# A layer with mLSTM recurrence on one core: the running maxima as rows through DRAM, a mask on GpSimd, and longer load estimates in the planner

## Chip, cores and metric

The kernel runs on one core of a Trainium2 chip. The metric is the device time of one execution in microseconds. The median of three runs is shown, and beside it the time of the one execution that the hardware profiler recorded. The engines are called TensorE (PE; its weight loads PEld), VectorE (DVE), ScalarE (ACT), GpSimd (POOL) and SyncE (SP), whose queue issues the DMA transfers.

## What is computed

One layer over 2048 tokens of width 1024 in float32, followed by a final norm. Two token mixers work side by side on one input projection: attention over a band of chunks (8 heads of 64), and an mLSTM, a matrix memory with exponential gates (4 heads of 128). Their outputs are gated and projected, and a feed-forward part of width 4096 follows. The change lies in the mLSTM. The part of the reference that matters, for one head:

```python
g = bcum + m_st[:, :, None]
dmat = bcum[:, :, :, None, :] - bcum[:, :, None, :, :] + ig[:, :, None, :, :]
dmat = jnp.where(causal[None, None, :, :, None], dmat, -jnp.inf)
m_t = jnp.maximum(g, jnp.max(dmat, axis=3))
dw = jnp.exp(dmat - m_t[:, :, :, None, :])
qk = jnp.einsum('bcthd,bcshd->bctsh', q, k) * dw
inter = jnp.exp(g - m_t)
num = (inter[..., None] * jnp.einsum('bchvk,bcthk->bcthv', c_st, q)
       + jnp.einsum('bctsh,bcshv->bcthv', qk, v))
den = inter * jnp.einsum('bchk,bcthk->bcth', n_st, q) + jnp.sum(qk, axis=3)
hout = num / jnp.maximum(jnp.abs(den), jnp.exp(-m_t))[..., None]
```

The weights `dw` form a triangle over source token s and target token t. After the cumulative sum of the target's forget gates cancels, each weight is the exponential of u(s) - m(t), where u belongs to the source and m is the target's running maximum.

## The kernel before

Tokens are worked in four blocks of 512 (`NB = 4`, `T = 512`), each cut into four chunks of 128 (`NT = 4`); the mLSTM uses chunks of 128 with the same result. Tiles hold features on the partitions and the 512 tokens of a block along the free dimension. Large products are made in three matmuls from operands that ScalarE and VectorE split into a high and a low part (L583 and L585 for weights, L1224 and L1229 for activations). Many of them are done as quads, a seven-product scheme for 2 by 2 blocks (L727), the others in the plain way (L644 to L646).

The program is written by a planner. Each piece of work is a Python generator, a thread, that yields requests: "pe", "act", "dve", "pool" or "sp" with an estimated duration (and, for transfers, an estimated time to landing), "get" for tiles of a pool, "wait" for events. `Flow.run` (L174) plays these threads against clocks of the engines and emits each instruction when its turn comes. The order in which TensorE's instructions are emitted is final. For threads with a priority below 5, TensorE's start is put `SLACK` = 800 ns behind the moment they are ready; the thread of the dense products has priority 5 and fills the list between them. Afterwards `Order` (L225) replays the whole program with its own durations and due times and settles the order on the other engines, SP's queue included. Each engine then executes its list in order; an instruction that waits holds up all that stands behind it.

The mLSTM of one block b goes as follows.

- `gates_rest` (L1493) makes, for 4 chunks x 4 heads, the sums of the gates, the sources' u (`sm["u"]`), the running maxima (`sm["mt"]`, 128 tokens x 16 columns) and their exponentials `ex`. At its end four transposes (L1580) bring the maxima into rows, a head to a partition, and a copy and a subtraction (L1582, L1585) split them into two parts in `mtt`. Then the event `gates` is set.
- `recurrence_far` (L1589) starts the heads; two are under way at most (`rec_room`). Each takes two tiles from `rpool`, two from `ctx` (the second of a head's tiles, `w`, holds the weights) and one from `temp`.
- `load_rec` (L1608) loads k, q and the values mv of a head, one after the other in the planner's reckoning (L1618, L1622).
- `rec_head` (L1655) waits for `gates`. It makes the exponents in a PSUM bank by two matmuls: L1663 puts the triangle's mask into it (identity times a bfloat16 mask), L1664 subtracts the maximum of each target by means of a column of `nsel` that picks the head's row of `mtt`. Four exponentials (L1668) read the bank, with u as the bias, and write `w`. Then come the transposes of k (L1675), its scaling by ScalarE (L1679), the products of k and q (L1686), their product with `w` on VectorE (L1688), and for each chunk three matmuls with the values and the state (L1700 to L1702) and the state's update (L1705).
- A square root is a power on GpSimd (L1722). GpSimd further scales the output gates of blocks 0 and 1 (L1652) and sets the edges of the attention's bias (L1324, L1325), and little else.

The recurrences of blocks 0 and 1 lie beside the input projections of these blocks, those of blocks 2 and 3 beside the first down projection; there they share tiles and banks with attention. The mixers' outputs go to DRAM (`mixd`, `mixa`), and `take_mix` (L961) brings them back for the projection (L989). A row is already spread over all partitions in other places: `row_out` (L1117) stores it to DRAM, and `row_in` (L1131) loads it with a source whose partition step is zero.

Of the kernel before, what the change touches and what calls it, by code (L numbers as in the profile page):

```python
# [30 lines left out]
P = 128  # L31
# [185 lines left out]
def dve_ns(n):  # L217
    return 70 + 1.042 * n
# [154 lines left out]
class Layer:  # L373
# [8 lines left out]
    def make_tiles(self, pool, psum):  # L382
# [8 lines left out]
        self.temp = Pool([f32(f"tmp{i}", 516) for i in range(6)])  # L391
# [6 lines left out]
        self.identb = pool.tile([P, P], BF16, name="identb")  # L398
        self.maskb = pool.tile([P, 1, P], BF16, name="maskb")
        self.gw = f32r("gw", KT + 4, 16)  # L400
        self.sel = f32("sel", 8)
# [7 lines left out]
        self.mtt = f32r("mtt", T)  # L409
        self.nsel = f32r("nsel", 8)  # L410
# [26 lines left out]
    def setup_late(self):  # L437
# [12 lines left out]
        nc.vector.memset(raw[:, :512], 0.0)  # L450
        nc.vector.tensor_copy(self.mtt, raw[:, :512])
        fl.put(self.temp, raw)
        yield "sp", 300, 2200
        nc.sync.dma_start(self.sel, io["sel"])
# [6 lines left out]
        nc.vector.tensor_copy(self.identb, self.ident)  # L461
        nc.vector.tensor_scalar(self.maskb[:, 0], self.tri, 1.0, -NEG, op0=ALU.subtract, op1=ALU.mult)
        nc.vector.tensor_scalar(self.nsel, self.sel, -1.0, None, op0=ALU.mult)
# [1029 lines left out]
    def gates_rest(self, b):  # L1493
# [84 lines left out]
        yield "pe", 428  # L1578
        for c in range(NT):
            nc.tensor.transpose(bk[:MH, c * P:(c + 1) * P], sm["mt"][:, c * MH:(c + 1) * MH], self.ident)  # L1580
        yield "act", act_ns(512, True)
        nc.scalar.copy(self.mtt[:MH], bk[:MH])  # L1582
# [25 lines left out]
    def load_rec(self, b, h):  # L1608
# [46 lines left out]
    def rec_head(self, b, h):  # L1655
# [5 lines left out]
        (bk,) = yield "get", self.banks, 1  # L1661
        yield "pe", 440
        mm(bk.rearrange("p (c t) -> p c t", c=NT), self.identb, self.maskb.to_broadcast([P, NT, P]), start=True, stop=False)  # L1663
        mm(bk, self.nsel[:, h:h + 1].to_broadcast([P, P]), self.mtt, start=False, stop=True)  # L1664
        for c in range(NT):
            n = c * MH + h
            yield "act", act_ns(128, True, 1)
            nc.scalar.activation(w[:, c * P:(c + 1) * P], bk[:, c * P:(c + 1) * P], AF.Exp,  # L1668
                                 bias=self.sm["u"][:, n:n + 1])
        fl.put(self.banks, bk)  # L1670
# [779 lines left out]
    def build(self):  # L2450
# [17 lines left out]
        self.rowd = {n: f32d("row" + n, T) for n in ("in1", "in2", "in3", "mid0", "mid1", "mid2", "mid3", "out0", "out1", "out2")}  # L2468
        self.wi = 0
# [17 lines left out]
        for b in range(NB):  # L2487
# [3 lines left out]
                gates=Event(), mv_slots=Event(), mv_ev=E(NT), ctx={}, mvh={}, ctx_ev=E(MH), qk_ev=E(2 * MH), og_ev=E(MH),  # L2491
# [14 lines left out]
def _layout(np, p):  # L2506
# [37 lines left out]
    sel = np.zeros((P, 8), np.float32)  # L2544
    for j in range(8):
        sel[j, j] = sel[32 + j, j] = 1.0
# [10 lines left out]
        sel=sel,  # L2557
# [29 lines left out]
```

## Time and profile before

| | us |
|---|---|
| median of three runs | 2779.6 (2778.0 to 2780.48) |
| the profiled execution | 2778.32 |
| its span, first to last instruction | 2776.5 |
| TensorE busy | 2751.0, 12994 matmuls |
| VectorE busy | 2057.1 |
| ScalarE busy | 1494.5 |
| GpSimd busy | 53.7 |

The granted TensorE clock was 0.998 of full speed. A row of a group reads: line, engine, operation, written tile, arrow, read tiles, shapes, count, then busy time, mean duration of one in ns, and the idle time of the engine just before these instructions. Matmuls overlap in such records, so a matmul's price in the stream is the distance from its start to the next start, not its duration. A row of the timeline reads: start, duration, engine, line, operation, tiles, count, and in brackets the idle time before it and what ended it. A row of the windows has the length of the stretch, the busy time of each engine with its number of instructions, the granted clock, the share of the DMA engines and the GB/s. For one line or tile the three numbers are the shortest, middle and longest duration in ns.

### The profile page before, as it was taken

To read this page: it belongs to the slowest core of one execution; us is meant where nothing else is said; L and a number is where in the kernel's file an instruction comes from. 1 tells how busy PE (TensorE), PEld (TensorE's weight loads), DVE (VectorE), ACT (ScalarE), POOL (GpSimd) and SP (SyncE) were. 2 spreads that over 40 slices of the span, in tenths; PEclk is the share of its full clock that TensorE was granted. 3 is DMA by queue.
4 is the path that set the end of the run, shared out by engine and by line. 5 is a ranking of instruction groups with operands and counts; after the bars stand their busy time and mean duration, and the time that the engine had idled before them with its cause. 6 is when DMAs were issued, how large, how long until landed. Compare 5 with 4: busy or idle time off the path is not lost.

```text
span 2776.5 us, 38600 instructions
## 1 busy us (share of the span) xinstructions
PE 2751.0 (99%) x12994; PEld 2286.5 (82%) x12994; DVE 2057.1 (74%) x3783; ACT 1494.5 (54%) x2608; POOL 53.7 (2%) x100
## 2 busy tenths in 40 slices
PE   9999999999999999999999999999999999999998
PEld 7888888888778878888888888888888888888887
DVE  7796789768996866886676688789888656556565
ACT  5564576535453535575555556565436655554443
POOL 0010001000000000000000000000000000000000
PEclk9999999999999999999999999999999999999999
DMA  7958759769755667579877887788777567666564
GB/s 273 291 195 276 230 166 304 250 222 319 262 199 204 220 243 256 198 270 325 288 280 273 287 245 233 230 256 253 251 261 261 206 220 261 243 238 217 189 230 149
DMA packets 329046, 678.64 MB, mean 244 GB/s; under 512 B 36840, under 2 KB 67728, under 8 KB 328848
## 3 DMA queue, kind: packets, MB, share of 16 engines
q1 hardware_dynamic: 328848, 676.18, 72.3%
q8 instruction: 102, 1.67, 0.2%
q14 instruction: 96, 0.79, 0.1%
HBM read 472.59 MB, written 203.44 MB: 243 GB/s over the span
## 4 chain that ended last, share of the span: by engine, by line
PE 91%; DMA 3%; DVE 3%; issue 2%; ACT 1%; SPq 0%; POOLq 0%; POOL 0%; DVEq 0%; ACTq 0%
PE bank L727 43%; PE bank L644 12%; PE bank L645 12%; PE bank L646 12%; PE bank L1415 2%; PE bank L1388 2%; PE bank L1446 2%; PE bank L755 2%; DVE wsp L585 1%; PE bank L1700 1%; PE bank L1701 1%; PE bank L1702 0%; PE bank L1686 0%; DMA wsum<-ctx 0%; ACT wsp L583 0%
## 5 line engine op out<-in xcount | busy, mean ns | idle before, releaser
L727 PE MATMUL bank<-r,wsp 128*128 128x512 f32 x5544 | 1265.5, 390 | 1.4 <-DVE ctx L1867 0.6
L727 PEld LDWEIGHTS bank<-r,wsp 128*128 128x128 f32 x5544 | 1038.0, 188 | 222.5 <-DVE ctx L1867 3.8
L585 DVE TENSOR_TENSOR wsp<-wraw,wsp 128x1024 fp32r<-128x1024 f32 x459 | 561.6, 1224 | 360.9 <-ACT wsp L583 335.2
L583 ACT CAST wsp<-wraw 128x1024 fp32r<-128x1024 f32 x459 | 482.5, 1052 | 464.1 <-PE bank L727 209.0
L644 PE MATMUL bank<-r,wsp 128*128 128x512 f32 x1472 | 586.1, 398 | 2.3 <-ACT r L1224 2.1
L645 PE MATMUL bank<-r,wsp 128*128 128x512 f32 x1472 | 574.8, 391 | 0.2 <-DVE r L1229 0.2
L646 PE MATMUL bank<-r,wsp 128*128 128x512 f32 x1472 | 574.9, 391 | 0.0
L646 PEld LDWEIGHTS bank<-r,wsp 128*128 128x128 f32 x1472 | 276.3, 188 | 58.7
L644 PEld LDWEIGHTS bank<-r,wsp 128*128 128x128 f32 x1472 | 276.9, 188 | 54.0 <-ACT r L1224 2.3
L645 PEld LDWEIGHTS bank<-r,wsp 128*128 128x128 f32 x1472 | 277.0, 188 | 50.5 <-DVE r L1229 0.5
L1867 DVE TENSOR_TENSOR ctx<-bank,ctx 128x512 f32<-128x512 f32 x186 | 127.1, 688 | 89.4 <-PE bank L727 89.2
L1229 DVE TENSOR_TENSOR r<-r 128x512 fp32r<-128x512 f32 x248 | 163.9, 687 | 25.3 <-ACT r L1224 24.5
L1224 ACT CAST r<-r 128x512 fp32r<-128x512 f32 x248 | 147.8, 624 | 49.8 <-DMA r<-u 47.0
L1859 ACT COPY ctx<-bank 128x512 f32<-128x512 f32 x186 | 107.9, 581 | 64.5 <-PE bank L727 60.9
L1430 ACT ACTIVATE sc<-sc,scs 128x640 f32<-128x640 f32 (+4 forms) x128 | 97.5, 763 | 71.7 <-DVE scs L1427 65.6
L2198 ACT ACTIVATE ctx<-ctx 128x512 f32<-128x512 f32 x96 | 60.6, 631 | 102.6 <-DVE ctx L1867 102.6
L1451 DVE TENSOR_TENSOR r<-bank,r 128x512 fp32r<-128x512 f32 (+1 forms) x168 | 97.1, 597 | 16.5 <-ACT r L1449 15.7
L1449 ACT CAST r<-bank 128x512 fp32r<-128x512 f32 (+1 forms) x168 | 81.8, 518 | 47.9 <-PE bank L1446 46.0
L1421 DVE CUSTOM_DVE_ANT_0 sc<-bank,bias 128x320 f32<-128x320 f32 (+3 forms) x240 | 103.7, 463 | 3.6 <-PE bank L1415 2.6
L1388 PE MATMUL bank<-r,r 128*128 128x512 f32 x336 | 96.0, 367 | 2.8 <-DVE r L1451 2.6
L602 DVE TENSOR_TENSOR wraw<-wraw,wraw 128x1024 f32<-128x1024 f32 x76 | 92.9, 1223 | 2.0
L552 DVE TENSOR_TENSOR ctx<-ctx,ctx 128x512 f32<-128x512 f32 x112 | 76.5, 688 | 17.7 <-DMA ctx<-in_wf 11.7
(258 smaller groups left out, 2720.7 us busy)
## 6 DMA issues: line engine op xcount, KB each, us to landing
wraw<-in_wf SPq DMA_DIRECT2D x178, 512.0 KB, 4.0
wraw<-wsum SPq DMA_DIRECT2D x136, 512.0 KB, 4.1
r<-u SPq DMA_DIRECT2D x224, 256.0 KB, 4.3
wraw<-in_w SPq DMA_DIRECT2D x88, 512.0 KB, 5.0
u<-ctx SPq DMA_DIRECT2D x128, 256.0 KB, 2.6
ctx<-in_wf SPq DMA_DIRECT2D x112, 256.0 KB, 4.3
wsum<-ctx SPq DMA_DIRECT2D x112, 256.0 KB, 3.6
u<-tmp SPq DMA_DIRECT2D x96, 256.0 KB, 3.7
```

Source lines behind the costliest of these rows:

```text
L583: nc.scalar.copy(w[:, 0], raw)
L585: nc.vector.tensor_sub(w[:, 1], raw, w[:, 0].bitcast(F32))
L644: mm(ps, lh, rh, start=first, stop=False)
L645: mm(ps, lh, rl, start=False, stop=False)
L646: mm(ps, ll, rh, start=False, stop=last)
L727: mm(ps, wv[:, x, k, n], a[:, y], start=new and k == 0 and x == y == 0, stop=k == 3 and x == 1, skip_group_check=True)
L1224: self.nc.scalar.copy(dst[:, 0], src)
L1229: self.nc.vector.tensor_sub(dst[:, 1], src, dst[:, 0].bitcast(F32))
L1388: nc.tensor.matmul(acc[:, :, c0:c0 + w], st, sl[:, :, o:o + w], start=n == 0, stop=n == total - 1)
L1421: nc.vector.tensor_tensor_reduce(out=e[:, x * w:x * w + w], in0=bks[x][:, :w], in1=br[:, j0 + x * w:j0 + x * w + w], op0=ALU.add, op1=ALU. ...
L1859: nc.scalar.copy(t[:, o:o + 512], ps)
L1867: nc.vector.tensor_add(t[:, o:o + 512], ps, t[:, o:o + 512])
```

## The change

The exponents are no longer made by TensorE. One transpose (of the maxima, sorted by head and chunk into 16 columns) replaces four, and ScalarE copies the result, 16 rows of 128, into one of the `cum` tiles, from where it goes to a DRAM tensor `rowm`, one for each block; only then is `gates` set. A new thread for each head, `row_rec`, waits for `gates`, loads the 512 maxima of the head from there into `w`, the same row on all partitions, and GpSimd adds a mask `later`, 1e30 where the target lies ahead of the source and 0 elsewhere. The four exponentials then read `w`, with a scale of -1 and u as the bias, and write in place. They stand, as before, ahead of the transposes of k in the head's thread, and now take no PSUM bank. The estimated time to landing for the head's loads goes from 2.0 to 4.5 us in the planner, and the pool of temporaries from six tiles to seven. `mtt`, `nsel`, `sel`, `identb` and `maskb` go, with their setup.

```diff
-        self.temp = Pool([f32(f"tmp{i}", 516) for i in range(6)])
+        self.temp = Pool([f32(f"tmp{i}", 516) for i in range(7)])
...
+        nc.vector.tensor_scalar(self.later[:, 0], self.tri, NEG, -NEG, op0=ALU.mult, op1=ALU.add)
...
-        yield "pe", 428
-        for c in range(NT):
-            nc.tensor.transpose(bk[:MH, c * P:(c + 1) * P], sm["mt"][:, c * MH:(c + 1) * MH], self.ident)
-        yield "act", act_ns(512, True)
-        nc.scalar.copy(self.mtt[:MH], bk[:MH])
-        yield "dve", dve_ns(512)
-        yield "dve", 85
-        V.tensor_sub(self.mtt[32:32 + MH], bk[:MH], self.mtt[:MH].bitcast(F32))
+        yield "dve", 85
+        V.tensor_copy(p.rearrange("p (m c) -> p m c", c=NT), v4("mt").rearrange("p c m -> p m c"))
+        yield "pe", 110
+        nc.tensor.transpose(bk[:16, 384:512], p, self.ident)
+        yield "act", act_ns(P, True)
+        nc.scalar.copy(z[:, 64:], bk[:16, 384:512])
         fl.put(self.banks, bk)
+        yield "sp", 900, 2000
+        nc.sync.dma_start(self.rowm[b].ap(), z[:, 64:])
         fl.set(B["gates"])
...
             fl.spawn(self.load_rec(b, h), 1)
+            fl.spawn(self.row_rec(b, h, B["ctx"][h][3]), 1)
             fl.spawn(self.rec_head(b, h), 1)
...
-            yield "sp", 900, 2000
+            yield "sp", 900, 4500
             nc.sync.dma_start(to[:, :512], self.mfar[b].ap()[x])
...
-        yield "sp", 900, 2000
+        yield "sp", 900, 4500
         nc.sync.dma_start(mvv[:, :, :128], self.mvfar[b].ap()[:, :, h * P:(h + 1) * P].rearrange("t p c -> p t c"))
...
+    def row_rec(self, b, h, w):
+
+        fl, nc, B = self.fl, self.nc, self.blk[b]
+        yield "wait", [B["gates"]]
+        yield "sp", 900, 4500
+        nc.sync.dma_start(w[:, :T], bass.AP(self.rowm[b], h * T, [[0, P], [1, T]]))
+        yield "pool", 730
+        w4 = w[:, :T].rearrange("p (c t) -> p c t", c=NT)
+        nc.gpsimd.tensor_tensor(w4, w4, self.later.to_broadcast([P, NT, P]), op=ALU.add)
+        fl.set(B["row_ev"][h])
...
         yield "wait", [B["gates"]]
-        (bk,) = yield "get", self.banks, 1
-        yield "pe", 440
-        mm(bk.rearrange("p (c t) -> p c t", c=NT), self.identb, self.maskb.to_broadcast([P, NT, P]), start=True, stop=False)
-        mm(bk, self.nsel[:, h:h + 1].to_broadcast([P, P]), self.mtt, start=False, stop=True)
+        yield "wait", [B["row_ev"][h]]
         for c in range(NT):
             n = c * MH + h
-            yield "act", act_ns(128, True, 1)
-            nc.scalar.activation(w[:, c * P:(c + 1) * P], bk[:, c * P:(c + 1) * P], AF.Exp,
+            yield "act", act_ns(128, False, 1)
+            nc.scalar.activation(w[:, c * P:(c + 1) * P], w[:, c * P:(c + 1) * P], AF.Exp, scale=-1.0,
                                  bias=self.sm["u"][:, n:n + 1])
-        fl.put(self.banks, bk)
         yield "wait", [B["qk_ev"][MH + h]]
```

More of the change, by code (lines that the diff above doesn't have):

```diff
@@ L397, in make_tiles @@
         self.ones = f32("ones", 2)
-        self.identb = pool.tile([P, P], BF16, name="identb")
-        self.maskb = pool.tile([P, 1, P], BF16, name="maskb")
+        self.later = f32("later", 1, P)
         self.gw = f32r("gw", KT + 4, 16)
-        self.sel = f32("sel", 8)
         self.bif = f32("bif", NT, 8)
@@ L2468, in build @@
         self.rowd = {n: f32d("row" + n, T) for n in ("in1", "in2", "in3", "mid0", "mid1", "mid2", "mid3", "out0", "out1", "out2")}
+        self.rowm = [f32d(f"rowm{b}", 16, P) for b in range(NB)]
         self.wi = 0
@@ L2490, in build @@
                 kq_ev=E(AH), q_ev=E(AH), k_ev=E(AH), k_spilt=E(AH), kq_all=Event(), head_done=E(AH),
-                gates=Event(), mv_slots=Event(), mv_ev=E(NT), ctx={}, mvh={}, ctx_ev=E(MH), qk_ev=E(2 * MH), og_ev=E(MH),
+                gates=Event(), mv_slots=Event(), mv_ev=E(NT), ctx={}, mvh={}, ctx_ev=E(MH), qk_ev=E(2 * MH), row_ev=E(MH), og_ev=E(MH),
                 mix=[None] * 8, mix_ev=E(8), ga={}, ga_ev=E(8), xs_free=Event(), x_room=E(KT), mid=Event(), vo={}, vn={}, vp_ev=E(4), mvh_ev=E(MH), gf=Event(), rec_slots={}, heads_left=[2] * 4))
@@ L2543, in _layout @@
     eye = np.eye(P, dtype=np.float32)
-    sel = np.zeros((P, 8), np.float32)
-    for j in range(8):
-        sel[j, j] = sel[32 + j, j] = 1.0
     cols = lambda v: v.reshape(-1, P).T
```

9 lines of the change are left out of this document (removed).

## The prediction, made before the changed kernel ran

> **What bounds the kernel now.** I read the page first, then who made TensorE wait, then the timeline around the instructions that the change removes. The page gives the span, the busy shares and the chain that ended last:
>
> ```profile
> span 2776.5 us, 38600 instructions
> PE 2751.0 (99%) x12994; PEld 2286.5 (82%) x12994; DVE 2057.1 (74%) x3783; ACT 1494.5 (54%) x2608; POOL 53.7 (2%) x100
> PE 91%; DMA 3%; DVE 3%; issue 2%; ACT 1%; SPq 0%; POOLq 0%; POOL 0%; DVEq 0%; ACTq 0%
> ```
>
> TensorE is the bound, 91% of the chain. Its stream is one fixed list in program order, so an instruction taken out of it is worth its start-to-start time wherever TensorE isn't waiting. The other engines come second, and matter where they make that list wait. These are the waits that the trace names ahead of matmuls (total us, times, longest):
>
> ```profile
> PE bank L644 <- ACT r L1180: 6.4, 1, 6.4
> PE bank L1388 <- DVE r L1451: 2.6, 2, 2.1
> PE bank L755 <- DVE ctx L1867: 2.4, 2, 2.0
> PE bank L644 <- ACT r L1224: 2.1, 1, 2.1
> PE bank L1700 <- DMA r<-mvfar: 0.7, 1, 0.7
> PE bank L727 <- DVE ctx L1867: 0.6, 1, 0.6
> ```
>
> The first is the start of the program, which the change doesn't touch. Of the rest, only L1700 is the recurrence waiting for its own load. The others (attention, the combining of the quads, the operands of the down projection) sum to 2.6 + 2.4 + 2.1 + 0.6 = 7.7 us.
>
> **Removed: the pair of matmuls for each head (L1663, L1664).** Here is one of the 16 pairs, with start and duration in us, and the two groups:
>
> ```profile
> 1835.72 0.39 PE L1663 MATMUL bank<-maskb,identb 128*128 128x512 bf16 x1
> 1835.76 0.58 PE L1664 MATMUL bank<-mtt,nsel 128*128 128x512 f32 x1
> 1836.18 0.39 PE L644 MATMUL bank<-r,wsp 128*128 128x512 f32 x1
> 1836.40 0.39 PE L645 MATMUL bank<-r,wsp 128*128 128x512 f32 x1
> ...
> L1664 PE MATMUL bank<-mtt,nsel 128*128 128x512 f32 x16 | 9.0, 583 | 0.0
> L1663 PE MATMUL bank<-maskb,identb 128*128 128x512 bf16 x16 | 6.2, 388 | 0.0
> ```
>
> Durations overlap, so I use starts: the next matmul starts 1836.18 - 1835.72 = 0.46 us after the pair begins, and runs at the usual 0.22 us from there. The last column of both groups is 0.0: TensorE wasn't idle ahead of them, so no wait swallows the saving. 16 x 0.46 = 7.4 us off the stream.
>
> **Removed: three of the four transposes of the running maxima, in each of four blocks.** Four transposes (L1580) become one of a tile with 16 columns, as L1534 has it:
>
> ```profile
> 67.92 0.60 PE L1580 MATMUL bank<-const,g_mt 128*4 128x128 f32 x4
> 68.28 0.48 PE L644 MATMUL bank<-r,wsp 128*128 128x512 f32 x1
> 68.59 0.39 PE L645 MATMUL bank<-r,wsp 128*128 128x512 f32 x1
> ...
> 55.62 0.27 PE L1534 MATMUL bank<-const,g_u 128*16 128x128 f32 x1
> 55.64 0.48 PE L644 MATMUL bank<-wsp,r 128*128 128x512 f32 x1
> 55.96 0.39 PE L645 MATMUL bank<-wsp,r 128*128 128x512 f32 x1
> ```
>
> From the group's start to L645 it is 0.67 us with four and 0.34 with one, and the L644 between them takes about 0.23 of it either way. The difference of 0.33 us, four times, is 1.3 us. On the other engines the block loses a copy and a subtraction of 4x512 and gains two small copies. VectorE (74% busy) and ScalarE (54%) aren't the bound, so that counts as nothing for the time.
>
> **Longer estimates for a head's loads.** They move no data. They make the planner place a head's matmuls later behind its loads, 4.5 us instead of 2.0. What they can win is the stall at L1700, where the load landed late:
>
> ```profile
> 452.39 0.39 PE L646 MATMUL bank<-r,wsp 128*128 128x512 f32 x1
> 453.52 0.46 PE L1700 MATMUL bank<-r,ctx 128*128 128x129 f32 x2 [0.74 <-DMA r<-mvfar]
> ```
>
> The starts lie 1.13 us apart instead of 0.23, so 0.9 us is to be had. I count 0.7, the wait itself: the loads of this kernel land in 4 to 5 us (next fence), so 4.5 covers the middle of them, not the worst.
>
> **Added: the rows.** A store per block, a load of 256 KB per head that spreads one row over 128 partitions, an addition of 128x512 on GpSimd, and the same four exponentials, now from SBUF. None of it is TensorE's. The nearest rows (L1133 is such a spread row, and the bottom line is its time to landing):
>
> ```profile
> L1133 SPq DMA_DIRECT2D tmp<-rowmid x8: 319/382/536, 1619.8 to 2684.1; - x8
> DMA to landing us min/median/max: 3.2/5.0/6.5
> ...
> r<-mfar SPq DMA_DIRECT2D x48, 256.0 KB, 4.7
> u<-ctx SPq DMA_DIRECT2D x128, 256.0 KB, 2.6
> ...
> L1652 POOL TENSOR_SCALAR ctx<-ctx,ghead x8: 1232/1759/2126, 197.2 to 453.1; 128x512 f32<-128x512 f32 x8
> ...
> L1668 ACT ACTIVATE ctx<-bank,g_u x64: 347/372/416, 73.1 to 1837.1; 128x128 f32<-128x128 f32 x64
> ```
>
> The chain of a head is then 5.0 (load) + 1.8 (addition) + 4 x 0.37 = 8.3 us at the middle. The planner reckons 0.9 + 4.5 + 0.73 + 4 x 0.29 = 7.3, and puts 0.8 us ahead of each of TensorE's instructions for such a thread. The addition with two inputs isn't in the trace: not below L1652's 1.2 us, and I bound it by twice L1652's longest, 4.3. The worst chain is 6.5 + 4.3 + 1.7 = 12.5 us, 4.4 beyond plan and margin. What hides this is the head's own loads: k, q and mv follow one another in the planner's reckoning, 3 x 5.4 = 16.2 us, and the weights are wanted only at L1700, after the last. That cover is missing where the gates come late and the loads lie far ahead, in the last block:
>
> ```profile
> 1778.62 0.58 ACT L1582 CAST mtt<-bank 4x512 fp32r<-4x512 f32 x1 [1.07 <-PE bank L1580]
> ...
> 1782.23 0.39 PE L1663 MATMUL bank<-maskb,identb 128*128 128x512 bf16 x1
> ...
> 1794.53 0.39 PE L1700 MATMUL bank<-r,ctx 128*128 128x129 f32 x2
> ```
>
> Now it is 16 us from the maxima to the first use of the weights. The store (about 2.6 us, as u<-ctx lands), the load and the addition go in between, and the planner moves these two heads' matmuls back; dense work fills the list meanwhile. Late by up to 4.4 us each, that is 0 to 9 us, and I take 0, since the middle exceeds the plan by 1.0 against a margin of 0.8. The 16 loads and 4 stores are 20 x 0.38 = 8 us of SP's issuing over the whole span, and the row's load is queued there behind the store that it must await, with all later transfers behind it. Spread rows exist already (L1133), and no matmul's wait in the list above names them. In GpSimd's queue the addition stands ahead of the power L1722 and the edges of the attention bias (L1324, L1325), and whoever waits for these waits for a late row too; I count nothing, GpSimd being 2% busy. ScalarE's exponentials, which awaited TensorE before, now await GpSimd. Behind them in ScalarE's list stand the copies of the weights (L583), for which VectorE's L585 and then the dense matmuls wait: a late row reaches TensorE on this way too, unless the three weight buffers ahead cover it.
>
> **The transfers' price where DMA is full.** In one stage it is:
>
> ```profile
> 1498.00:1560.00 62.00, 59.71 (x281) 49.23 (x281) 32.58 (x54) 31.36 (x58) 1.01 (x1) 1.00 1.01 336
> ```
>
> The DMA share is 1.01 (second last) at 336 GB/s, and TensorE loses 2.3 us, most of it the L644 wait for r behind a late load. The first two heads of block 2 load here. Two rows of 256 KB at 336 GB/s are 1.6 us. Bounds: 0 if the rows come before the crowd, 1.6 if they delay the load that TensorE awaits. I take 1.6, as nothing is free there.
>
> **Sum**, against the profiled execution of 2778.3 us (span 2776.5 and 1.8 around it): 2778.3 - 7.4 - 1.3 - 0.7 + 1.6 = 2770.5. That execution is 1.3 us below the median of the runs, 2779.6, so the forecast for a median is 2771.8, say 2772.
>
> **The rivals.**
> *The rows come late at every head (slower).* Place: L1700 (through L1688's product) of all 16 heads, in a list that can't overtake. For it: the addition's price is unknown and its plan (0.73 us) is below anything L1652 shows. Against it: 16.2 us of loads beside 7.3. The forecast's 7.8 us are gone from 0.5 us per head, and it is slower by more than can be told from no change from 0.8. L1652's middle and longest lie 1.0 and 1.4 us over the plan. If the margin is already spent on the loads, that is 16 to 22 us, 19 in the middle: 2791. Chance 0.13.
>
> *Attention finishes late.* Heads that stay longer hold tiles and PSUM banks that attention of blocks 2 and 3 wants, and their last tile has little slack ahead of the projection that ends at 2070.7:
>
> ```profile
> 2021.42 0.69 DVE L1229 TENSOR_TENSOR r<-tmp,r 128x512 fp32r<-128x512 f32 x1
> ...
> 2070.73 183.03 PE bank L727 x807
> ```
>
> Block 3's projection is 64 products of 0.68 us, 44 us, so it starts near 2027 and wants this fourth tile at 2029; it is ready at 2022.1. Slack 6 to 7 us. With a head in the last block some 7.5 us longer (3 x 2.5), two in a row 15, the end could slip by 15 and cost 8: 2780. Against it: the recurrence takes no bank for its mask any more, and one more tile in the temporaries' pool. Chance 0.09.
>
> *GpSimd holds VectorE up.* While GpSimd ran L1652, a subtraction that takes 1.22 us took 1.60:
>
> ```profile
> 215.30 3.56 POOL L1652 TENSOR_SCALAR ctx<-ctx,ghead 128x512 f32<-128x512 f32 x2 [9.27 <-ACT ctx L1649]
> ...
> 216.17 1.60 DVE L585 TENSOR_TENSOR wsp<-wraw,wsp 128x1024 fp32r<-128x1024 f32 x1
> ...
> L585 DVE TENSOR_TENSOR wsp<-wraw,wsp x459: 1214/1225/1600, 5.1 to 2746.4; 128x1024 fp32r<-128x1024 f32 x153
> ```
>
> At 0.38 us for each of 16 additions, all of it reaching TensorE, it is 6 us: 2778. VectorE's 26% idle speaks against all of it reaching TensorE. Chance 0.07. The Trainium skill, "SBUF — State Buffer", section "Who interferes with whom", says that a VectorE instruction with two SBUF inputs and a GpSimd instruction that reads SBUF exclude each other for the whole instruction. By that rule VectorE could be held for a whole addition each time, an estimate of 16 x 1.76 = 28 us, and 2800 if all of it reached TensorE; the 1.60 agrees in direction, with 0.38 us held instead of 1.76.
>
> *The order is drawn anew.* Every edit changes the planner's list for the whole program, so the 7.7 us of stalls elsewhere come out differently: half of them gone gives 2768, inside the forecast; three times as many 2787, which I give 0.07; most of them gone, and small losses with them, 2763, 0.08.
>
> *No relief*, since TensorE would have waited anyway: the 0.0 beside L1663 and L1664 speaks against it. 0.04, 2779.
>
> **How the numbers follow.** About 0.2%, 5.6 us, is what a measurement of this kernel tells from no change: faster ends at 2774. The forecast (2766 to 2774 on its own) has 0.52. Faster: 0.52 and the good draw's 0.08, with 0.02 from the mild ends of attention and GpSimd, 0.62. Within: the rest of these two, no relief and a part of a bad draw, 0.20. Slower: late rows and the worse part of a bad draw, 0.18. The range goes from 2761, a good draw, to 2787, the bad one, and leaves out late rows at their middle.
>
> **What would show it.** Right: no L1663 or L1664, TensorE's matmuls 44 fewer, waits ahead of L1700 and L644 no longer than now. Wrong: waits ahead of L1700 that name w's chain (ScalarE's exponentials or VectorE's product), waits in the projection before 2070 for tiles of attention, L585 far above 1.23 us beside additions, or new waits of 2 us in places the recurrence has nothing to do with.

## The result, and the profile after

| | before | after |
|---|---|---|
| median, us | 2779.3 (2778.0 to 2780.5, 6 runs) | 2795.3 (2790.1 to 2799.6, 6 runs) |
| the profiled execution, us | 2778.32 | 2795.56 |
| its span, us | 2776.5 | 2793.6 |
| TensorE's matmuls | 12994 | 12950 |

The changed kernel is slower: the ratio of its runs to those of the kernel before is 1.0052, 95% interval 1.0038 to 1.0065, and the medians are 16.0 us apart, where 7.8 us less had been forecast; 2795.3 lies above the range. The 44 matmuls are gone, as the page shows, and TensorE is busy for 98% of its span instead of 99%. VectorE and ScalarE hardly changed, GpSimd has its 16 additions more, and the mean of the weight splits on VectorE (L576, before L585) is nearly as it was, 1226 ns after 1224.

```profile
span 2793.6 us, 38551 instructions
PE 2750.2 (98%) x12950; PEld 2285.1 (82%) x12950; DVE 2061.9 (74%) x3779; ACT 1498.5 (54%) x2608; POOL 70.4 (3%) x116
PE 88%; DMA 4%; DVE 4%; issue 2%; ACT 1%; SPq 0%; POOL 0%; POOLq 0%; DVEq 0%; ACTq 0%
...
L576 DVE TENSOR_TENSOR wsp<-wraw,wsp 128x1024 fp32r<-128x1024 f32 x459 | 562.8, 1226 | 358.2 <-ACT wsp L574 339.2
```

In the chain of what ended last, TensorE falls from 91% to 88%: the time is in waits. These are the waits ahead of matmuls after the change (total us, times, longest). Lines have shifted: L635 is L644 of before, L1379 L1388, L746 L755, L1674 and L1685 are the transposes of k and the products of k and q.

```profile
PE bank L635 <- ACT r L1171: 6.7, 1, 6.7
PE bank L1379 <- DVE r L1442: 6.2, 2, 5.7
PE bank L635 <- ACT r L1215: 5.7, 2, 5.3
PE bank L1674 <- DMA r<-mfar: 2.8, 2, 2.6
PE bank L746 <- DVE ctx L1866: 2.6, 2, 2.2
PE bank L1685 <- DMA r<-mfar: 2.3, 1, 2.3
PE bank L635 <- DVE ctx L1978: 1.8, 1, 1.8
```

The first is the start of the program again. Without it, all the waits that the two views name sum to 27.1 us after and 9.9 before. Two stand out, 5.7 and 5.3 us, and two kinds are new, a head's own k and q coming late (2.8 and 2.3).

To separate waits from work, I take the distance from each matmul's start to the next, and call *excess* what it has over the usual distance of the same two forms. The span without the excess is the length of TensorE's list itself.

| profiled execution | span | excess | list without it |
|---|---|---|---|
| before | 2776.5 | 40.7 | 2735.8 |
| after | 2793.6 | 65.3 | 2728.3 |

So the list became 7.5 us shorter, and 24.6 us of standing and slow matmuls were added: -7.5 + 24.6 = 17.1, the difference of the spans. The choice of what counts as the same form moves these values by about 1 us.

The 5.3 us wait shows how. Here is the timeline of the changed kernel around it, cut to the row, ScalarE and the matmuls on both sides of the wait:

```profile
1556.51 0.50 SPq L1622 DMA_DIRECT2D ctx<-rowm  x1
...
1560.28 0.31 ACT L1753 ACTIVATE tmp<-tmp 128x128 f32<-128x128 f32 x1 [0.36 <-DVE tmp L1749]
...
1561.60 0.83 PE L1406 MATMUL bank<-r,r 128*128 128x320 f32 x4
...
1563.42 1.26 POOL L1625 TENSOR_TENSOR ctx<-ctx,later 128x512 f32<-128x512 f32 x1 [49.81 <-DMA ctx<-rowm]
1564.72 1.28 ACT L1668 ACTIVATE ctx<-ctx,g_u 128x128 f32<-128x128 f32 x4 [4.03 <-POOL ctx L1625]
...
1565.90 1.03 ACT L574 CAST wsp<-wraw 128x1024 fp32r<-128x1024 f32 x1
...
1567.10 2.17 ACT L1215 CAST r<-r 128x512 fp32r<-128x512 f32 x4
...
1567.76 2.07 PE L635 MATMUL bank<-r,wsp 128*128 128x512 f32 x4 [5.33 <-ACT r L1215]
```

The row is issued at 1556.5 and has landed by 1563.4, and GpSimd adds the mask. ScalarE stands still for 4.03 us, because the head's exponentials (L1668) are next in its list. Behind them stand a weight copy (L574), a short activation and L1215, which splits an operand of the dense product. TensorE's next matmul needs that operand. The view names L1215 as the one that TensorE waits for; one has to look at what ScalarE did before it to find the row. No matmul of the head itself waits here.

The additions and the rows as groups, in the views of their line and of the DRAM rows (shortest, middle and longest; ns for the addition, us for the landing):

```profile
L1625 POOL TENSOR_TENSOR ctx<-ctx,later x16: 1262/1406/1837, 90.1 to 1895.4; 128x512 f32<-128x512 f32 x16
...
who waited for it (us, times):
  ACT ctx L1668: 14.2, 9
```

```profile
L1622 SPq DMA_DIRECT2D ctx<-rowm x16: 319/428/496, 79.6 to 1889.8; - x16
...
DMA to landing us min/median/max: 3.9/6.2/7.2
```

ScalarE stood 14.2 us in 9 places for additions. `Order` (L225), which writes ScalarE's list, reckons 1.4 + 0.65 + 1.1 = 3.15 us for the row and keeps a margin of 2.5 behind a transfer, so that the exponentials may stand 5.65 us behind the row's issue; the addition's 0.73 falls into that margin, since the replay lets it start at the landing. Here the chip took 1564.72 - 1556.51 = 8.2 us, and ScalarE was there after 4.2.

The 5.7 us wait, at 111.26 us, is of another kind. The timeline of the same kernel there:

```profile
104.53 1.05 PE L1437 MATMUL bank<-const,sc 128*128 128x128 f32 x6
...
109.61 0.63 ACT L1066 ACTIVATE ctx<-ctx 128x512 f32<-128x512 f32 x1 [6.09 <-DMA ctx<-in_xt]
...
110.15 0.95 ACT L1440 CAST r<-bank 128x384 fp32r<-128x384 f32 x2
...
111.26 1.01 PE L1379 MATMUL bank<-r,r 128*128 128x512 f32 x2 [5.68 <-DVE r L1442]
```

ScalarE stands for a load of the input this time, with attention's copy L1440 behind. No row is awaited here. ScalarE stands from 103.5 us on and the load is issued at 104.4; another place in the newly drawn list would explain it, but no run tests this one wait.

After such waits the matmuls run slower for a while. TensorE's timeline behind the 5.3 us wait:

```profile
1569.63 0.63 PE L636 MATMUL bank<-r,wsp 128*128 128x512 f32 x1
1570.05 0.63 PE L637 MATMUL bank<-r,wsp 128*128 128x512 f32 x1
1570.48 0.63 PE L635 MATMUL bank<-r,wsp 128*128 128x512 f32 x1
...
1573.22 0.39 PE L636 MATMUL bank<-r,wsp 128*128 128x512 f32 x1
1573.45 0.39 PE L637 MATMUL bank<-r,wsp 128*128 128x512 f32 x1
```

The starts lie 0.43 us apart, later 0.23. Counted over the profile, matmuls that start late within 8 us behind a stall of over 1 us cost 8.9 us after and 3.0 before. Of the 24.6 us, 27.1 - 9.9 = 17.2 are named waits, 5.9 are these slow matmuls, and 1.5 are smaller things.

### The profile page after: what moved, and what is told of

It is laid out like the page before. It is cut to its first block, busy times and chain, and to the rows that moved or that the text cites. A ratio compares the mean times of both kernels' runs of the same rounds, so it can differ in the third digit from the quotient of the medians.

```text
span 2793.6 us, 38551 instructions
## 1 busy us (share of the span) xinstructions
PE 2750.2 (98%) x12950; PEld 2285.1 (82%) x12950; DVE 2061.9 (74%) x3779; ACT 1498.5 (54%) x2608; POOL 70.4 (3%) x116
## 4 chain that ended last, share of the span: by engine, by line
PE 88%; DMA 4%; DVE 4%; issue 2%; ACT 1%; SPq 0%; POOL 0%; POOLq 0%; DVEq 0%; ACTq 0%
PE bank L718 43%; PE bank L635 11%; PE bank L636 11%; PE bank L637 11%; PE bank L1406 2%; PE bank L746 2%; PE bank L1379 2%; PE bank L1437 2%; DMA r<-mfar 1%; DVE wsp L576 1%; DMA ctx<-rowm 1%; DMA r<-mix 1%; PE bank L1685 1%; DMA wsum<-ctx 0%; DMA r<-u 0%
## 5 line engine op out<-in xcount | busy, mean ns | idle before, releaser
L576 DVE TENSOR_TENSOR wsp<-wraw,wsp 128x1024 fp32r<-128x1024 f32 x459 | 562.8, 1226 | 358.2 <-ACT wsp L574 339.2
L574 ACT CAST wsp<-wraw 128x1024 fp32r<-128x1024 f32 x459 | 483.1, 1052 | 468.0 <-PE bank L718 201.7
L635 PE MATMUL bank<-r,wsp 128*128 128x512 f32 x1472 | 587.8, 400 | 6.3 <-ACT r L1215 5.7
L637 PE MATMUL bank<-r,wsp 128*128 128x512 f32 x1472 | 576.3, 392 | 0.0
L635 PEld LDWEIGHTS bank<-r,wsp 128*128 128x128 f32 x1472 | 277.7, 189 | 58.7 <-ACT r L1215 6.4
L637 PEld LDWEIGHTS bank<-r,wsp 128*128 128x128 f32 x1472 | 277.2, 188 | 59.3
L1220 DVE TENSOR_TENSOR r<-r 128x512 fp32r<-128x512 f32 x248 | 165.1, 692 | 30.8 <-ACT r L1215 30.0
L1215 ACT CAST r<-r 128x512 fp32r<-128x512 f32 x248 | 149.1, 623 | 61.2 <-DMA r<-u 56.0
L1412 DVE CUSTOM_DVE_ANT_0 sc<-bank,bias 128x320 f32<-128x320 f32 (+3 forms) x240 | 103.5, 463 | 12.3 <-PE bank L1406 12.0
L1379 PE MATMUL bank<-r,r 128*128 128x512 f32 (+1 forms) x336 | 95.1, 365 | 6.2 <-DVE r L1442 6.2
L1440 ACT CAST r<-bank 128x512 fp32r<-128x512 f32 (+1 forms) x168 | 81.0, 517 | 36.2 <-PE bank L1437 31.6
```

The source lines that it names most:

```text
L574: nc.scalar.copy(w[:, 0], raw)
L576: nc.vector.tensor_sub(w[:, 1], raw, w[:, 0].bitcast(F32))
L635: mm(ps, lh, rh, start=first, stop=False)
L637: mm(ps, ll, rh, start=False, stop=last)
L1215: self.nc.scalar.copy(dst[:, 0], src)
L1220: self.nc.vector.tensor_sub(dst[:, 1], src, dst[:, 0].bitcast(F32))
```

## The experiments

Seventeen kernels ran. The table has, beside the two kernels, each one's median, its ratio to the kernel before on the same chip, and from its profiled execution the span, the excess, the list without it, the part of the excess between 400 and 500 us, and ScalarE's waits for additions. The profiled execution needn't be a typical one: where it is some us below the median (the rows with * lie 3.5 us or more below), the excess is of that quick execution.

```
                      median  ratio interval     span   excess  list  400-500  additions
before                2779.3                    2776.5  40.7  2735.8   3.7
 slack 790            2783.3  1.0002 to 1.0021  2784.4  49.1  2735.3   5.4
 slack 810            2783.7  1.0007 to 1.0025  2781.6  47.2  2734.4   5.4
 FAR 4500        *    2782.7  1.0004 to 1.0023  2776.4  40.4  2736.0   2.9
 long loads           2787.5  1.0020 to 1.0043  2787.0  51.6  2735.4   8.7
 pair twice           2784.7  1.0011 to 1.0030  2782.6  39.7  2742.9   2.6
after                 2795.3  1.0038 to 1.0065  2793.6  65.3  2728.3  10.5     14.2
 slack 790            2794.2  1.0043 to 1.0073  2796.8  68.8  2728.0  13.6     18.7
 short loads     *    2794.9  1.0043 to 1.0077  2788.9  62.2  2726.7  11.7     22.8
 late exps       *    2791.3  1.0030 to 1.0060  2784.5  58.2  2726.3   8.7     24.4
 six tmp              2792.6  1.0037 to 1.0064  2789.8  61.2  2728.6  13.1     14.3
measured rows    *    2787.8  1.0024 to 1.0054  2781.1  53.6  2727.5  14.1      0.0
 late exps            2788.2  1.0025 to 1.0051  2784.1  57.0  2727.1   7.8      0.2
 short loads          2794.7  1.0040 to 1.0070  2792.8  65.4  2727.4  13.6      2.2
 FAR 4500             2786.5  1.0011 to 1.0032  2787.1  60.0  2727.1   7.9      0.8
 slack 780       *    2786.5  1.0014 to 1.0037  2780.4  52.8  2727.6  10.2      1.9
 slack 790       *    2786.3  1.0013 to 1.0036  2779.9  52.7  2727.2   9.6      2.0
 slack 810            2781.1  1.0002 to 1.0021  2778.8  50.8  2728.0   7.6      2.3
 slack 820            2793.2  1.0037 to 1.0063  2787.6  60.7  2726.9  17.6      2.0
```

The column "list" has three groups of values in it: 2734.4 to 2736.0 for the kernel with the pairs, 2726.3 to 2728.6 without them, 2742.9 with them made twice.

**Empty edits, and the load estimates apart from the rest.** `SLACK` only decides where the planner puts instructions.

```diff
-    SLACK = 800.0
+    SLACK = 790.0
```

> The kernel before with the planner's slack ahead of TensorE at 790 ns instead of 800: nothing but the drawn order changes. Theory D (every edit draws a new order, and the order before was a lucky one): 5 to 25 us slower than before, stalls in places that differ from those of before. Theory L (the heads' long estimates) and theory R (the rows hold up ScalarE and TensorE): within 4 us of before, either way.

> The changed kernel with the same 790 ns. Theory D: moves by 5 us or more from 2795, either way, and its long stalls lie elsewhere than in the changed kernel. Theories L and R: within 4 us of 2795, with stalls again at the heads' loads (L) or behind exponentials that await the additions (R).

The estimates of k and q (L1618) and of mv (L1622), long in the kernel before and, the other way round, short in the changed one:

```diff
-            yield "sp", 900, 2000
+            yield "sp", 900, 4500
```

> The kernel before with 4.5 us for the heads' three loads instead of 2.0, and nothing else. Theory L: 8 to 16 us slower than before, 2788 to 2795, with new stalls at the heads' loads. Theory R: within 4 us of before. Theory D: anything from 2775 to 2800, not tied to the heads' loads.

> The changed kernel with 2.0 us again for k, q and mv (4.5 stays for the new row). Theory L: the saving of 8.7 us of matmuls shows, 2768 to 2776. Theory R: stays near 2790 to 2798, the longest stall again behind exponentials that wait for an addition. Theory D: anything from 2775 to 2800.

An edit that means nothing costs the kernel before 3.8 us (2783.3 against 2779.5 on that chip) and leaves the changed one where it was. So the changed kernel's 16 us hardly are the luck of one list, but a few of them are the luck of the other: the list before was a good one. The longer estimates alone cost 8 us against that good list. Their waits show that the loads come late instead of early:

```profile
PE bank L1675 <- DMA r<-mfar: 3.8, 1, 3.8
PE bank L1388 <- DVE r L1451: 3.4, 4, 2.8
```

The 0.7 us that L1700 waited for mv is gone, and the transposes of k wait 3.8. But taken back in the changed kernel they bring nothing (2794.9 against 2795.3), so the two effects don't add, and this isn't the cause of the 16 us.

**What the pair was worth, and three remedies for the rows.** First the pair of matmuls made twice in the kernel before, with no cost in the planner (a few lines of `Order`, not shown), so that the other lists stay nearly as they are:

```diff
 mm(bk.rearrange("p (c t) -> p c t", c=NT), self.identb, self.maskb.to_broadcast([P, NT, P]), start=True, stop=False)
 mm(bk, self.nsel[:, h:h + 1].to_broadcast([P, P]), self.mtt, start=False, stop=True)
+mm(bk.rearrange("p (c t) -> p c t", c=NT), self.identb, self.maskb.to_broadcast([P, NT, P]), start=True, stop=False)
+mm(bk, self.nsel[:, h:h + 1].to_broadcast([P, P]), self.mtt, start=False, stop=True)
```

> The kernel before with each of the 16 pairs of mask matmuls made twice; the second pair costs nothing in the planner, so the lists of all engines stay as before but for a dozen exchanged neighbours. If the pair is worth 0.46 us of TensorE's list, as the prediction reckoned: 16 x 0.46 = 7.4 us more, 2787 (2785 to 2789). If TensorE would have waited there anyway: 2780.

The list is 2742.9 - 2735.8 = 7.1 us longer, with the excess as it was (39.7 and 40.7). That is the 7.4 of the prediction. The median says 4.9 (2784.7 against 2779.8), a little under the 2785 expected at the least.

Then the planner gets times for row and addition that go by the measured ones: in `Order` 3.15 + 4.0 = 7.15 us to landing (the longest row took 7.2), in `Flow` 7.0, and 1.5 for the addition (middle 1.41). The first line of the edit also gives 1.5 us to GpSimd's scaling of the output gates. The lists with this edit are called those with measured rows.

```diff
-            return 1200.0 if n <= 8 else 80 + 1.27 * n
+            return 1200.0 if n <= 8 else 1500.0 if n >= 512 else 80 + 1.27 * n
...
+                if any(x.tensor.name.startswith("rowm") for x in self.operands(self.ins[k].ins)):
+                    end += 4000.0
...
-        yield "sp", 900, 4500
+        yield "sp", 900, 7000
...
-        yield "pool", 730
+        yield "pool", 1500
```

> The changed kernel with the row's true price in the planner: 4 us more to landing and 1.5 us for the addition, so that ScalarE's list has the exponentials later. Theory R (ScalarE's list stands still behind exponentials that await the addition, 14 us in all in the changed kernel, and the stall of TensorE near 1565 us is one of these): these waits of ScalarE fall under 4 us in all, the stall near 1565 falls from 5.5 to about 3 us, and the time to 2778 to 2788. Theory D (the draw alone): the waits may fall, but the time stays within 4 us of 2795 or goes anywhere.

Or the exponentials go behind the transposes and the scaling of k in the head's thread, without and with those estimates:

```diff
         yield "wait", [B["gates"]]
-        yield "wait", [B["row_ev"][h]]
-        for c in range(NT):
-            n = c * MH + h
-            yield "act", act_ns(128, False, 1)
-            nc.scalar.activation(w[:, c * P:(c + 1) * P], w[:, c * P:(c + 1) * P], AF.Exp, scale=-1.0,
-                                 bias=self.sm["u"][:, n:n + 1])
...
+        yield "wait", [B["row_ev"][h]]
+        for c in range(NT):
+            n = c * MH + h
+            yield "act", act_ns(128, False, 1)
+            nc.scalar.activation(w[:, c * P:(c + 1) * P], w[:, c * P:(c + 1) * P], AF.Exp, scale=-1.0,
+                                 bias=self.sm["u"][:, n:n + 1])
```

> The changed kernel with the wait for the row and the exponentials behind the scaling of k instead of ahead of k's transposes. Theory R: the rows have 2 to 3 us more, ScalarE's waits for additions shrink from 14 us, and the time is 4 to 10 us below 2795. Theory D: within 4 us of 2795 or anywhere, with ScalarE's waits no guide to it.

> Both edits together. Theory R: no wait of ScalarE for an addition above 1 us, 2774 to 2786. Theory D: no better than a_honest or a_late alone, 2785 to 2800.

With measured times nobody on ScalarE waits for an addition any more, and the kernel gains 7.5 us (2795.3 to 2787.8). The views of its addition and of its waits:

```profile
L1627 POOL TENSOR_TENSOR ctx<-ctx,later x16: 1264/1301/1913, 85.5 to 1894.0; 128x512 f32<-128x512 f32 x16
...
who waited for it (us, times):
  PEld bank L1701: 1.1, 1
  PE bank L1701: 0.8, 1
```

```profile
PE bank L1687 <- DMA r<-mfar: 7.6, 2, 5.4
PE bank L637 <- ACT r L1173: 6.7, 1, 6.7
PE bank L637 <- ACT r L1217: 2.7, 1, 2.7
```

The wait that was 5.3 us (here L637 for L1217) is 2.7, near the 2.1 of before. What is left is a head's k and q (L1687), 7.6 us. Putting the exponentials later was expected to shorten ScalarE's waits; they grew to 24.4 us, with 7.0 at one place, while the time fell by 4.0. With both edits it is 2788.2, where 2774 to 2786 was expected, no better than with measured estimates alone. So the planner's estimate of the row matters; that the order within the thread does isn't shown. ScalarE's waits in sum are no measure of the time, though: lists with measured rows and 2 us of them run at 2781.1 as well as at 2793.2.

**What is left over the kernel before.** Short estimates for k, q and mv beside measured ones for the row; then `FAR`, by which `Order` brings a transfer forward of its use, at 4.5 us instead of 2.5, in both kernels; and one more empty edit of the kernel before, `SLACK` 810.

```diff
-    REACH, LAND, FAR = 1400.0, 1100.0, 2500.0
+    REACH, LAND, FAR = 1400.0, 1100.0, 4500.0
```

> a_honest with 2.0 us again for k, q and mv. Theory C (the longer heads push the second pair of heads of block 1 into the crowd of transfers near 450 us, where their loads are late by up to 5.5 us): the stalls between 400 and 500 us fall from 14 to under 8 us, and the time to 2774 to 2784. Theory S (short estimates make TensorE wait at the loads instead): as many stalls or more, with L1687's and L1701's waits for r<-mfar and r<-mvfar, 2786 to 2794.

> a_honest with transfers due 4.5 instead of 2.5 us ahead of their use in the second planning (FAR). If the loads are late because SP issues them late: the waits of TensorE for r<-mfar fall from 8 us under 3, 2776 to 2784. If they are late because the transfers crowd at that point: these waits stay, 2785 to 2795.

> The kernel before with 810 ns of slack, a second empty edit. Theory D (the order before was a lucky draw): slower again, as the 790 ns were, by 2 to 10 us. If it was not lucky: within 2 us of before or faster.

> The kernel before with FAR at 4.5 us, the control to a_hfar. If earlier transfers help as such, whatever the change: 2770 to 2777. If they only repair what the rows brought: 2778 to 2786.

Short estimates are 6.9 us worse beside measured rows, so they are no remedy. Much of it lies in one place: the excess from 1490 to 1600 is 11.7 us against 4.7, and there the wait for L1217's operand is 8.8 us instead of 2.7, with ScalarE standing for a load of weights:

```profile
1557.65 1.04 ACT L576 CAST wsp<-wraw 128x1024 fp32r<-128x1024 f32 x1 [6.64 <-DMA wraw<-in_wf]
```

One list doesn't show that the short estimates bring this about. `FAR` brings TensorE's waits for k and q down from 8.7 us to 2.9, and the stretch from 400 to 500 us from 14.1 to 7.9, as was expected if SP issues these loads late; but other waits come in their place, and the median gains only 1.3, to 2786.5 where 2776 to 2784 was expected. The second empty edit costs 5.3 us.

Four empty edits of the kernel with measured rows, to see how much of its 8 us is luck:

> The rows with the measured estimates (2787.8 us, span 1 us longer than its own profile of 2781) and SLACK 780 in place of 800: an edit that means nothing, so that the order of the list is drawn anew. Theory 'drawn anew': what is left over the kernel before (8 us) is the luck of two lists, so the four redraws scatter on both sides of 2783 (what empty edits of the kernel before gave), with at least one at or below 2780, and the excess of TensorE's spacing falls to 45 us or less in that one. Theory 'crowded stage': the second pair of heads of blocks 0 and 1 has its loads too late in any list; all four lie between 2785 and 2792, each with 6 us or more of excess in the stretch from 400 to 500 us.

> As the one with 780, with SLACK 790. Theory 'drawn anew': one of four values scattered from 2778 to 2790. Theory 'crowded stage': 2785 to 2792, with 6 us or more of excess from 400 to 500 us.

> As the one with 780, with SLACK 810. Theory 'drawn anew': one of four values scattered from 2778 to 2790. Theory 'crowded stage': 2785 to 2792, with 6 us or more of excess from 400 to 500 us.

> As the one with 780, with SLACK 820. Theory 'drawn anew': one of four values scattered from 2778 to 2790. Theory 'crowded stage': 2785 to 2792, with 6 us or more of excess from 400 to 500 us. ScalarE's waits for the additions stay below 3 us in all four by either theory, since the planner has their measured times.

Neither theory holds alone. The draws scatter by 12 us, from 2781.1 to 2793.2, so luck matters. But none is below the kernel before, and in all five lists the stretch from 400 to 500 us has 7.6 to 17.6 us of excess, where the four lists with the pairs and short estimates have 2.9 to 5.4. The rows and the long load estimates both stand in these five; each seems to raise the stretch by itself, 8.7 us with long loads and no rows, 11.7 and 13.6 with rows and short loads. The worst draw shows what TensorE awaits, in its waits and its timeline:

```profile
PE bank L1687 <- DMA r<-mfar: 7.8, 1, 7.8
PE bank L1676 <- DMA r<-mfar: 6.6, 4, 2.9
```

```profile
455.63 0.38 SPq L2121 DMA_DIRECT2D mfar<-ctx  x1
456.07 0.42 SPq L1612 DMA_DIRECT2D r<-mfar  x1
456.54 0.43 SPq L1624 DMA_DIRECT2D ctx<-rowm  x1
...
463.11 1.22 PE L1687 MATMUL bank<-r 128*128 128x128 f32 x4 [7.79 <-DMA r<-mfar]
```

The last of q's and k's loads is issued at 456.07, and TensorE has been waiting since 463.11 - 7.79 = 455.32. So the load was late before it began; it then took 7 us, the upper end of what such loads take (before: 3.0, 4.9, 7.5). Here SP had been issuing one transfer after another. That the rows and their longer stay make the second pair of heads come too late in this stage is my reading; no run took it away with the rows kept.

Last the seventh tile of temporaries, taken back:

```diff
-        self.temp = Pool([f32(f"tmp{i}", 516) for i in range(7)])
+        self.temp = Pool([f32(f"tmp{i}", 516) for i in range(6)])
```

> The changed kernel with six tiles of temporaries instead of seven; rows, additions and estimates as in the change. If the seventh tile was worth something, this is slower than the changed kernel by over 3 us (2799 or more). If it is worth nothing, it is another draw of the list of the changed kernel: 2791 to 2799, with ScalarE's waits for the additions between 12 and 25 us as in the other lists with the short estimates for the rows. If the seventh tile was itself what brought the list out of order, 2788 or less.

It is another draw with short estimates for the rows (2792.6, waits of 14.3 us), so the tile isn't the cause.

**One wait in all lists.** Where the changed kernel has its 5.3 us wait, TensorE waits in every list for ScalarE's split of an operand of the down projection (L1215, before L1224). The table has this wait and what ScalarE stood for just ahead of the split, from the profiled executions:

| lists | TensorE's wait, us | ScalarE stood for |
|---|---|---|
| pairs: before, slack 790, slack 810, FAR | 2.1, 2.5, 0.7, 1.1 | the load of r, 4.5 to 6.4 |
| pairs, long loads | 3.0 | the load of r, 3.8 |
| rows with the change's estimates: after, slack 790, short loads, late exps, six tmp | 5.3, 7.1, 5.7, 7.7, 5.7 | an addition, 4.0 to 7.0 |
| measured rows: the first, late exps, FAR, slack 780, 790, 810, 820 | 2.7, 3.2, 4.0, 4.8, 4.5, 3.8, 3.5 | the load of r, 2.4 to 3.8 |
| measured rows, short loads | 8.8 | a load of weights, 6.6, then r, 2.9 |

In all five lists that reckon the row short, ScalarE stands for an addition at this place, and in no other list. The wait is 6.3 us in the mean there and 3.8 with measured rows and long loads, and the longest of the latter (4.8) lies below the shortest of the former (5.3). So what a row reckoned short costs is shown at this place beyond the luck of a draw: some 2.5 us. With the pairs the mean of the five is 1.9; some 2 us stay with the rows even when they are reckoned rightly, and why isn't shown.

**What the runs add up to.** I take means over lists of one kind. With the pairs and the short load estimates: 2779.3, 2783.3, 2783.7, 2782.7, mean 2782.3. Changed, with the change's own estimates for rows: 2795.3, 2794.2, 2794.9, 2791.3, 2792.6, mean 2793.7. Changed, with measured rows and the long load estimates: 2787.8 and the four draws, mean 2787.0. The 16.0 us are then some 3.0 of a good draw before, 4.7 for rows that are reckoned rightly, 6.7 for rows reckoned wrongly, and 1.6 of a poor draw after. The 4.7 is what is lost over and above the 7.5 us saved. Single draws lie up to 6 us from their mean, so the second and third number have an uncertainty of about 2 us each, and they hang on which lists are counted: with all eight that have measured rows (2788.2, 2794.7 and 2786.5 too) their mean is 2788.0, and both numbers are 5.7. No kernel beat the one before.

## Why the prediction was wrong

**The bound and the savings were right.** A matmul out of TensorE's list is worth its distance: 8.7 us for pairs and transposes was forecast, 7.5 went in the changed kernel, and the pair doubled cost 7.1 against 7.4. "No relief" is out.

**The failed step is the lateness of the rows: "I take 0", and "I count nothing" for the queues.** The chain was sized well: 5.0 + 1.8 + 1.5 us at the middle was the forecast, 6.2 + 1.4 + 1.3 the measurement. It was held against the wrong reckoning and the wrong waiter. I compared it with the 7.3 us and 0.8 us of `Flow`, which places TensorE's instructions, and asked whether the weights reach L1700 in time. There the cover was good: 16.2 us of loads hide the chain, and in the changed kernel no wait ahead of that matmul (now L1699) reaches 0.2 us. But ScalarE's list is written by `Order`, which allows 5.65 us, margin included, from the row's issue to the exponentials. The exponentials stand in ScalarE's list too early, and everything behind them waits, dense operands among it. The text named this way and the copies behind, and then let "unless the three weight buffers ahead cover it" stand as an answer. In the longest of these waits it wasn't the weight copy that TensorE awaited but L1215, the split of an activation, behind it in the list. A price could have been had from rows on hand: 5.0 + 1.8 = 6.8 us is 1.15 us of ScalarE's standing for each of 16 heads at the middle, and 6.5 + 4.3 = 10.8 is 5.15 us at the worst, so 18 to 82 us on ScalarE. With the measured 6.2 + 1.4 it is 1.95 us, 31 in all; 14.2 came, in 9 places, and measured estimates gave back some 6 us of time.

**The term of the load estimates was wrong in sign, or at best nothing.** L1700's 0.7 us went, and k and q came late for 2.8 + 2.3. Alone in the kernel before, the estimate gave 2787.5, 3.8 us above the worst of the four lists with short ones: a loss, if not a draw worse than any seen. Beside the rows, taking it back changed nothing with the change's estimates and cost 6.9 us with measured ones, in one list each.

**The transfers' 1.6 us in the full stage** can't be told from the rest in the changed kernel. From 1495 to 1570 us the DMA share was 1.00 at 339 GB/s before and 0.98 at 323 after, and ScalarE's wait for the row hides the load. With measured rows the wait there is some 2 us longer than with the pairs, near the 1.6, but that the rows' transfers delay the load isn't shown.

```profile
200.00:240.00 40.00, 37.36 (x198) 31.43 (x197) 33.03 (x79) 23.64 (x57) 7.99 (x10) 0.96 0.91 299
465.00:500.00 35.00, 31.48 (x148) 25.39 (x149) 29.31 (x61) 23.41 (x57) 3.15 (x2) 0.95 0.90 305
1495.00:1570.00 75.00, 69.67 (x322) 58.07 (x321) 42.27 (x57) 41.53 (x78) 4.24 (x3) 0.97 0.98 323
```

These are windows of the changed kernel (length, busy time of TensorE, its weight loads, VectorE, ScalarE and GpSimd with instructions, granted clock, DMA share, GB/s). For two of them, the kernel before:

```profile
465.00:500.00 35.00, 34.94 (x177) 29.13 (x176) 31.66 (x60) 27.12 (x61) 4.14 (x3) 1.00 0.92 328
1495.00:1570.00 75.00, 72.71 (x345) 60.35 (x344) 42.70 (x81) 39.26 (x74) 1.01 (x1) 1.00 1.00 339
```

TensorE is busy 31.48 us of 35 from 465 on, where it was 34.94; the granted clock is 0.95 to 0.97 in these stages with long waits.

**A term was missing:** a stall's price isn't its length. The slow matmuls behind the waits are 5.9 us of the loss.

**The rivals.** "The rows come late at every head" had the origin, but named L1700 as the place; the rows came late for ScalarE. That its 2791 is near the time is luck in part, since only some 6 of the 16 us are theirs. "The order is drawn anew" was real, but not as far as its 2787: it explains 3.0 + 1.6 us. "Attention finishes late" didn't happen: from 2000 us on the excess is 2.1 us, before 1.3. "GpSimd holds VectorE up" is real on VectorE. The mean of L576 hides it (1226 ns, middle 1225, longest of 459 2306). But eight VectorE instructions that ran beside an addition took 0.4 to 1.1 us longer than the middle of their kind, 7.4 us in all where the rival had 6, and none without GpSimd beside it took over 0.4 us longer. Here is one (L1220 takes 686 ns at the middle):

```profile
1512.33 1.29 POOL L1625 TENSOR_TENSOR ctx<-ctx,later 128x512 f32<-128x512 f32 x1 [12.76 <-DVE r L1220]
1512.44 1.72 DVE L1220 TENSOR_TENSOR r<-r 128x512 fp32r<-128x512 f32 x1 [0.15 <-ACT r L1215]
```

How much of it reached TensorE isn't shown: of its waits that begin within 5 us behind these instructions, two are put down to VectorE, 0.3 and 1.8 us. The Trainium skill, "SBUF — State Buffer", "Who interferes with whom", would let 16 additions of 1.4 us hold VectorE for 22 us, an estimate for the case that each meets an instruction with two SBUF inputs. The trace agrees in kind, with 7.4 us: seven of the eight have two such inputs.

## What to carry to other kernels

Before a change moves work into a chain through other engines and DRAM, hold the chain's measured length against the number by which each engine's list is written, not only against the last consumer: in a list that can't overtake, the price is paid by whatever stands behind. When a planner orders the whole program, give every new step its measured time, and redraw both kernels with empty edits before a few us are put down to the change. One wait compared over all the lists can show what the medians leave open. Look behind the instruction that a wait names, at what its engine did before it.

## What was unexpected of the hardware

In these two profiles a wait of 2 us or more on TensorE is mostly followed by 8 to 12 matmuls that start up to 0.2 us later than usual, 1.2 to 1.8 us on top, but two nearly equal waits of the kernel before, in its timeline of TensorE, differ: behind the first such matmuls cost 1.7 us, behind the second 0.2.

```profile
975.66 5.50 PE L755 MATMUL bank<-wsp,r 128*128 128x512 f32 x16 [1.98 <-DVE ctx L1867]
...
1550.34 0.49 PE L644 MATMUL bank<-r,wsp 128*128 128x512 f32 x1 [2.06 <-ACT r L1224]
```

The granted clock (third column from the right) tells them apart, in the windows behind the two waits:

```profile
976.08:979.49 3.41, 3.41 (x10) 2.63 (x9) 3.38 (x5) 0.00 (x0) 0.00 (x0) 0.50 1.04 410
1550.34:1553.75 3.41, 3.17 (x14) 2.39 (x15) 3.15 (x5) 2.46 (x4) 0.00 (x0) 1.00 1.05 400
```

Behind the first wait the clock is 0.50 for 3.41 us, and the matmuls of that stretch are the slow ones; behind the second it stays at 1.00. The Trainium skill, "TensorE: Matmul & The Clock Gate", Part 1, has a free-running window of about 3.4 us, and half the clock after a window in which TensorE was idle. The trace agrees in the clock and in the length, and the unequal prices would fit a window that doesn't start with the wait; that a wait of 1.98 us, shorter than a window, suffices is this trace's own.

GpSimd's addition of two 128x512 inputs took 1.26 to 1.84 us, middle 1.41, and a spread row of 256 KB 6.2 us to land at the middle, where L1133's rows before took 5.0.
